# Ordering VectorE's weight work behind the gate chain and the residual additions at the out-projection openings of two FFNs, and reordering products of each first chunk

## The chip, the cores and the metric

One NeuronCore of a Trainium2 chip runs the whole kernel. The metric is the device time of one execution in microseconds (us). A separate execution was recorded by the hardware profiler; all rows of the profile come from it, and its times are counted from the first instruction. The engines are TensorE (PE, with its weight loads PEld), VectorE (DVE), ScalarE (ACT), GpSimd (POOL) and SyncE (SP), which issues most loads.

## The reference

The reference is one step of a two-layer streaming encoder over 512 prompt frames and 8 x 16 sample frames, 640 columns in all. Layer 0 is a Conformer convolution module, layer 1 attends to a shared K/V, and each is followed by a SwiGLU FFN. Everything is float32. Only the FFN matters here, with 1024 features and a hidden width of 2816:

```
def swiglu_ffn(h, g, w_in, w_out):
    a, b = jnp.split(rms_norm(h, g) @ w_in, 2, axis=-1)
    return h + (jax.nn.silu(a) * b) @ w_out
```

It is computed twice, once after each layer.

## The kernel before, in words

Features lie on the 128 partitions, frames along the rows. TensorE takes each float32 operand as two parts, `hi` (rounded to float32r) and `lo` (the rest), and a product of two is three matmuls: hi times hi, lo times hi, hi times lo (`product`, L436 to L445, matmul at L443). So every tile of weights must first be "cut": ScalarE writes hi (L375), VectorE subtracts to get lo (L376, `put`, L374). The gated values go through the same `put`; by their tiles the rows are told apart: `whi`, `wlo`, `shi`, `slo` are weights, `hid` gated values and `XH`, `XL` the FFN's input.

Most of each FFN multiplies 2 x 2 blocks with seven products instead of eight, named X11, X21, XT1, XT2, XT3, XT4 and X22. `w_seven` (L414) fetches one set of weights for that. SP loads four blocks into `raw` (two buffers); GpSimd loads one block into `s1` and adds another to it by DMA (L421, L422; two buffers too). Then VectorE makes sums in place, L426 (a21 = a11 + a21), L427 (a11 = s1 + a11) and L429 (a12 = a12 + a11), and each of the seven results is cut into a slot. There are 11 slots, used in turn.

Both FFNs (`ffn`, L337) go through 18 of the 22 tiles of hidden rows in three chunks. A chunk first has calls of `seven` (L528): six, but three in the first chunk, where three calls of another kind (`std`) stand ahead. A call makes a = W_a x and b = W_b x for one tile of hidden rows: 12 matmuls for each of the seven products. Products X11, XT2, XT3 and XT4 of a call add up in one accumulator, and ScalarE copies it out in between (`keep`, L455, after X11, XT2 and XT3). X21 is added to the first copy (`plus`, L460). Silu follows (L464), and the gate (`sink`, L502) multiplies (L480, L483), forms the sums that the second matrix needs (L483, L514, L522) and puts them into `hid`. The last two products of a call, XT4 and X22 (`after`, L546), are held over into the next call, or into the out-projection.

Then `out_chunk` (L559) multiplies the gated values of this chunk by its part of w_out, in four weight sets u = 0 to 3, again with seven products each, 9 matmuls in a product (three tiles of hidden rows, three matmuls each). Each finished accumulator is added to or subtracted from the residual `h` by VectorE (L584). The order on TensorE is written out by hand:

```
QORD = """50' a0 a1 10' 50" 10" 20 60' 30' 51' 60" 30" 51" 70 11 21 40 61 31 52 71 12 22 41 62 32 53 72
          13 23 42 63 33"""
```

The first digit is the product (5 XT1, 1 X11, 2 X21, 6 XT2, 3 X22, 7 XT3, 4 XT4), the second is u. One quote mark is the first six matmuls of the nine, two are the last three, which need the newest tile of hidden rows. `a0` and `a1` are the held-over XT4 and X22 of the last call (12 matmuls each); the last gated values come only from them. Products 7 and 4 of u = 3 (73, 43) are left for the first call of the next chunk. I call the stretch from 50' to about 70 the opening. Weights for u are fetched when QORD first names that u.

What is not written out by hand is ordered by a planner at compile time. It lists each engine's instructions by priority and by a model of when they are ready; `high_priority` raises a block. `tc.issue_after(i)` (in a helper, `behind`, L140) adds an edge: those instructions of the block that run on the same engine as `i` are listed after it. It is an order within one engine and adds no semaphore wait by itself. At run time each engine follows its list.

Of the kernel before, what the change touches and what calls it, by code (L numbers as in the profile page):

```python
# [60 lines left out]
X11, X21, XT2, XT1, XT3, XT4, X22 = range(7)  # L61
# [24 lines left out]
def tile_trunk(ctx, tc, xT, vecs, hist, w_pw1, w_pw2, w_in0, w_out0, w_os0, w_in1, w_out1, w_os1,  # L86
               w_kq, w_v, w_o, rel, kc, vc, y_out, convp_out, convs_out, k_out, v_out):
    nc = tc.nc
# [15 lines left out]
    def nm(s):  # L104
        uid[0] += 1
        return f"{s}_{uid[0]}"

    def mmt(n=512):
        return mm.tile([P, n], F32, tag="mm", name=nm("mm"))
# [29 lines left out]
    @contextmanager  # L139
    def behind(*ins):  # L140
        with ExitStack() as st:
            for i in ins:
                st.enter_context(tc.issue_after(i))
            yield
# [192 lines left out]
    def ffn(l, w_in, w_out, w_os, tail, hf, lead=(), b0=None, last_sum=()):  # L337
# [19 lines left out]
        lead, put_end = list(lead), [None, None]  # L357

        def ties():
            return lead.pop(0) if lead else ()  # L360
# [5 lines left out]
        sub, add, mult = ALU.subtract, ALU.add, ALU.mult  # L366
# [7 lines left out]
        def put(hi, lo, src):  # L374
            put_end[1] = nc.scalar.activation(out=hi, in_=src, func=AF.Copy).ins  # L375
            put_end[0] = nc.vector.tensor_tensor(out=lo, in0=src, in1=hi.bitcast(F32), op=sub).ins  # L376

        def cut(w, o, src):
            c = slice(o, o + src.shape[-1])
            put(w[0][:, c], w[1][:, c], src)  # L380

        def wraw():
            return wp.tile([P, 2048], F32, tag="raw", name=nm("raw"))
# [9 lines left out]
        def slot():  # L393
            turn[0] += 1
            hi, lo, o = slots[(turn[0] - 1) % len(slots)]
            return (hi, lo), o
# [14 lines left out]
                            cut(*ws[j // 512], raw[:, j:j + n])  # L411
            return ws[1], ws[0], ws[2], ws[3]

        def w_seven(src, out=False, first=(), rest=()):  # L414
            n = src.shape[-1] // 4
            raw, ws = wraw(), {}
            s1 = wx.tile([P, 512], F32, tag="s1", name=nm("s1"))[:, :n]
            nc.sync.dma_start(raw[:, :4 * n], src)
            a12, a11, a21, a22 = (raw[:, n * i:n * i + n] for i in range(4))
            with tc.high_priority(offset=HP), behind(*ties()):  # L420
                nc.gpsimd.dma_start(s1, src[:, 2 * n:3 * n])  # L421
                nc.gpsimd.dma_start(s1, src[:, 3 * n:4 * n], accum_op=add)  # L422
                for x in ((XT1, X11, X21, XT2, X22, XT3, XT4) if out else
                          (X11, X21, XT2, XT1, XT3, XT4, X22)):
                    if x == XT2:
                        nc.vector.tensor_tensor(out=a21, in0=a11, in1=a21, op=add)  # L426
                        nc.vector.tensor_tensor(out=a11, in0=s1, in1=a11, op=add)  # L427
                    elif x == X22:
                        nc.vector.tensor_tensor(out=a12, in0=a12, in1=a11, op=add)  # L429
                    ws[x] = slot()  # L430
                    with behind(*(first if x == XT1 else rest)):
                        cut(*ws[x], {XT1: s1, X11: a11, X21: a12, XT2: a11, X22: a12, XT3: a21,
                                     XT4: a22}[x])
            return ws

        def product(pt, w, xs, first, ks=None):  # L436
            (hi, lo), o0 = w
            n = len(xs)
            for k in ks or range(n):
                xh, xl = xs[k]  # L440
                c = slice(o0 + k * P, o0 + k * P + P)
                for i, (wt, v) in enumerate(((hi[:, c], xh), (lo[:, c], xh), (hi[:, c], xl))):
                    last = nc.tensor.matmul(pt, wt, v, start=(first and k == i == 0),  # L443
                                            stop=(k == n - 1 and i == 2), skip_group_check=True)
            return last  # L445

        def xproduct(pt, w, x, first):
            return product(pt, w, [(XH[x][:, k, :], XL[x][:, k, :]) for k in range(4)], first)

        keeps = []  # L450

        def keep(tag, pt):
            t = tp.tile([P, NH], F32, tag=tag, name=nm(tag))
            with tc.high_priority(offset=HP):
                keeps.append(nc.scalar.activation(out=t, in_=pt, func=AF.Copy).ins)  # L455
            return t

        def plus(t, pt):
            with tc.high_priority(offset=HP):
                nc.vector.tensor_tensor(out=t, in0=pt, in1=t, op=add)  # L460

        def silu(t, src):
            with tc.high_priority(offset=HP):
                nc.scalar.activation(out=t, in_=src, func=AF.Silu)  # L464
# [27 lines left out]
        def combined(HH, HL, kp, second, held, neg, early=None):  # L492
# [32 lines left out]
                        own(XT4, b21)  # L525
            return sink

        def seven(src, sink, before):  # L528
            ws = w_seven(src)
            pa, pb = mmt()[:, :NH], mmt()[:, :NH]  # L530
            xproduct(pa, ws[X11], X11, True)
            t1 = keep("t1", pa)
            before(0)
            xproduct(pb, ws[X21], X21, True)
            plus(t1, pb)
            silu(t1, t1)
            before(1)
            xproduct(pa, ws[XT2], XT2, False)
            t2 = keep("t2", pa)
            pe = mmt()[:, :NH]  # L540
            xproduct(pe, ws[XT1], XT1, True)
            xproduct(pa, ws[XT3], XT3, False)
            t3 = keep("t3", pa)
            plus(t3, pe)

            def after(i):  # L546
                if i == 0:
                    last = xproduct(pa, ws[XT4], XT4, False)
                    sink(0, t1, pa)
                else:  # L550
                    last = xproduct(pe, ws[X22], X22, False)
                    plus(t2, pe)
                    silu(t2, t2)
                    sink(1, t2, t3)
                return last

            return after

        def out_chunk(c, HH, HL, after):  # L559
            ws, pts = {}, {}  # L560
            prod = {5: ("e", XT1, True, 1, 1), 1: ("a", X11, True, 0, 0),
                    2: ("b", X21, True, 0, 0), 6: ("a", XT2, False, 1, 0),
                    3: ("e", X22, False, 1, 0), 7: ("a", XT3, False, 1, 1),
                    4: ("a", XT4, False, 0, 1)}

            def go(i, u, part):
                if u not in ws:
                    o = (4 * c + u) * 12 * P
                    ws[u] = w_seven(w_os[:, o:o + 12 * P], True,
                                    (keeps[2:3], keeps[-2:-1])[u] if c == 0 and u < 2 else (),  # L570
                                    keeps[-1:] if (c, u) == (0, 1) else ())
                b, x, first, half, row = prod[i]
                if first and part != '"':
                    pts[b, u] = mmt()[:, :NH]
                pt = pts[b, u]
                with tc.issue_after(last[0]) if last else nullcontext():
                    ins = product(pt, ws[u][x], list(zip(HH[x], HL[x])), first,
                                  {"": None, "'": (0, 1), '"': (2,)}[part])
                last[:] = [ins.ins]
                if part == "'":  # L580
                    return
                hv = h[:, 2 * u + row, half * NH:half * NH + NH]
                with tc.high_priority(offset=HP):
                    nc.vector.tensor_tensor(out=hv, in0=hv, in1=pt, op=sub if row else add)  # L584

            last = []
            for t in QORD.split():
                if t[0] == "a":
                    with tc.issue_after(last[0]):
                        last[:] = [after(int(t[1])).ins]  # L590
                else:
                    go(int(t[0]), int(t[1]), t[2:])
            return lambda i: go((7, 4)[i], 3, "")

        def stats(half):
            bc, _ = rstd_bc([h[:, k, half * NH:half * NH + NH] for k in range(KT)], NH, SQ, 6, None,
# [76 lines left out]
        for c in range(NCH):  # L673
            for jj in range(NSTD if c == 0 else 0, CW):
                if jj % 2 == 0:
                    held = [None] * 3
                if jj == NSTD and c == 0:
                    held = helds[1]
                after = seven(w_in[CW * c + jj], combined(HH, HL, jj // 2, jj % 2, held, True),
                              after)  # L680
            after = out_chunk(c, HH, HL, after)
            HH, HL = {}, {}
# [888 lines left out]
    for p in range(NP):  # L1571
# [8 lines left out]
        for op in BO[p].split():  # L1580
# [11 lines left out]
            i = int(op[1]) if len(op) > 1 else None  # L1592
            with pe(), tc.high_priority(offset=HP):
                if op[0] == "A":
# [4 lines left out]
                    pt = {hh: sp.tile([P, 1280], F32, tag="PT", name=nm("PT")) for hh in range(2)}  # L1599
# [22 lines left out]
    with tc.high_priority(offset=HP):  # L1622
        sqs = xp.tile([P, KT, 384], F32, tag="xl1", name=nm("sqs")).rearrange("p a n -> p (a n)")
        acc, r = sqs[:, KT * NH:(KT + 1) * NH], sqs[:, (KT + 1) * NH:(KT + 1) * NH + 8]
        for k in range(KT):
            sq = square(h[:, k, 0:NH], NH, "a", sqs[:, k * NH:(k + 1) * NH])
            if k:
                sq_end = nc.vector.tensor_tensor(out=acc, in0=acc if k > 1 else sqs[:, 0:NH],
                                                 in1=sq, op=ALU.add).ins
# [100 lines left out]
    last = [next(products) for _ in range(KT)][-1:]  # L1730
# [116 lines left out]
```

## Time and profile before

| what | value |
|---|---|
| time, median of 3 runs | 1443.44 us (1442.41 to 1444.12) |
| the profiled execution | 1440.09 us, span of its instructions 1438.3 us |
| TensorE busy | 1417.7 us (99% of the span), 11076 matmuls |
| VectorE busy | 1116.5 us (78%), 2490 instructions |
| ScalarE busy | 749.4 us (52%) |
| granted TensorE clock | 0.999 of full speed |

The first FFN runs from about 240 to 650 us of the span, the second from about 1000 to 1415. In a profile row the first number is the start, the second the duration, then engine, line, operation, output and inputs; in square brackets stands the time that the engine sat idle before it, and what ended that. In the list of waits a row gives who waited for whom, the total in us, how often, and the longest. Matmuls are pipelined: one of 128 x 320 is recorded as 0.31 us long though the next starts half as long after it.

### The profile page before, as it was taken

The page shows a single profiled execution, that of the slowest core. Times are in us where ns is not written, and L with a number is a line of the kernel's source. Part 1 is how long each engine was busy: PE and PEld are TensorE (multiplying, and loading weights), DVE is VectorE, ACT ScalarE, POOL GpSimd, SP SyncE. Part 2 cuts the span into 40 slices and gives each one's busy share as a digit, 9 for nine tenths or more (in the row PEclk, how much of TensorE's full clock was granted, in tenths as well). Part 3 has the DMA queues.
Part 4 walks back from the last instruction along what each step waited for, and adds up shares of the span by engine and source line. Part 5 has one row for each costly group of instructions (what it writes and reads, how often), then busy time and mean ns, then how long its engine had stood idle before and what let it go on. Part 6 is the DMA issues. An engine that isn't in the chain of part 4 may idle for free. (4 is left out here: it accounts for less than half of the span.)

```text
span 1438.3 us, 28229 instructions
## 1 busy us (share of the span) xinstructions
PE 1417.7 (99%) x11076; PEld 1363.5 (95%) x11076; DVE 1116.5 (78%) x2490; ACT 749.4 (52%) x1633; POOL 278.8 (19%) x335
## 2 busy tenths in 40 slices
PE   9999999999999999999999999999999999999998
PEld 9998799999999999999998998988999999999998
DVE  6799767988888889766666757667899788888855
ACT  5666554554554554545654544544564564554443
POOL 5699120011111111013111111110011111111101
PEclk9999999999999999999999999999999999999999
DMA  7267434055444445424455555561044534544512
GB/s 247 97 171 183 123 87 148 9 142 150 135 101 127 132 116 138 128 89 173 164 184 201 188 182 173 182 214 61 30 107 137 153 109 119 135 117 127 144 59 74
DMA packets 66933, 192.58 MB, mean 134 GB/s; under 512 B 12144, under 2 KB 30320, under 8 KB 58480
## 3 DMA queue, kind: packets, MB, share of 16 engines
q1 hardware_dynamic: 52432, 160.58, 34.4%
q0 software_dynamic: 13504, 29.37, 10.3%
q8 instruction: 87, 1.43, 0.4%
q10 hardware_dynamic: 864, 0.83, 0.2%
q14 instruction: 46, 0.38, 0.1%
HBM read 179.14 MB, written 11.61 MB: 133 GB/s over the span
## 5 line engine op out<-in xcount | busy, mean ns | idle before, releaser
L443 PE MATMUL mm<-XH,whi 128*128 128x320 f32 x896 | 275.6, 310 | 2.6 <-ACT t L455 2.6
L443 PE MATMUL mm<-XH,wlo 128*128 128x320 f32 x896 | 276.3, 309 | 0.0
L443 PE MATMUL mm<-XL,whi 128*128 128x320 f32 x896 | 274.7, 309 | 0.0
L375 ACT ACTIVATE whi<-raw 128x512 fp32r<-128x512 f32 (+2 forms) x280 | 169.0, 614 | 139.7 <-PE mm L443 113.3
L376 DVE TENSOR_TENSOR wlo<-raw,whi 128x512 fp32r<-128x512 f32 (+2 forms) x280 | 184.2, 666 | 21.2 <-ACT whi L375 20.2
L443 PE MATMUL mm<-hid,whi 128*128 128x320 f32 x732 | 171.9, 310 | 3.4 <-DVE hid L376 2.7
L443 PEld LDWEIGHTS mm<-XH,whi 128*128 128x128 f32 x896 | 167.8, 188 | 4.2 <-ACT t L455 4.2
L443 PEld LDWEIGHTS mm<-XH,wlo 128*128 128x128 f32 x896 | 168.2, 188 | 0.0
L443 PEld LDWEIGHTS mm<-XL,whi 128*128 128x128 f32 x896 | 167.8, 188 | 0.0
L443 PEld LDWEIGHTS mm<-hid,whi 128*128 128x128 f32 x732 | 124.8, 188 | 6.0 <-DVE hid L376 3.7
L202 PE MATMUL mm<-xh,whi 128*128 128x320 f32 (+2 forms) x416 | 128.8, 312 | 0.8 <-DVE h L706 0.4
L203 PE MATMUL mm<-xh,wlo 128*128 128x320 f32 (+2 forms) x416 | 128.0, 309 | 0.0
L204 PE MATMUL mm<-xl,whi 128*128 128x320 f32 (+2 forms) x416 | 125.6, 310 | 0.4 <-DVE xl L192 0.4
L443 PE MATMUL mm<-hid,wlo 128*128 128x320 f32 x366 | 113.0, 309 | 0.0
L443 PE MATMUL mm<-XH,shi 128*128 128x320 f32 x344 | 105.9, 309 | 0.7 <-DVE h L1560 0.7
L443 PE MATMUL mm<-XH,slo 128*128 128x320 f32 x344 | 106.0, 308 | 0.0
L443 PE MATMUL mm<-XL,shi 128*128 128x320 f32 x344 | 105.5, 308 | 0.0
L421 POOL DMA_DIRECT2D s<-in_w_in x38 | 22.0, 579 | 374.3 <-DVE wlo L376 149.7
L852 POOL TENSOR_TENSOR ca<-ca,cvt 128x512 f32<-128x512 f32 x60 | 89.7, 1494 | 17.0 <-ACT cvt L849 10.8
L375 ACT ACTIVATE shi<-raw 128x512 fp32r<-128x512 f32 (+1 forms) x114 | 66.4, 588 | 43.9 <-PE mm L443 39.0
L455 ACT ACTIVATE t<-mm 128x320 f32<-128x320 f32 x114 | 49.6, 435 | 67.3 <-PE mm L443 66.6
L584 DVE TENSOR_TENSOR h<-h,mm 128x320 f32<-128x320 f32 x168 | 79.6, 479 | 4.9 <-PE mm L443 4.7
(337 smaller groups left out, 3683.4 us busy)
## 6 DMA issues: line engine op xcount, KB each, us to landing
raw<-in_w_in SPq DMA_DIRECT2D x38, 1024.0 KB
s<-in_w_in POOLq DMA_DIRECT2D x76, 256.0 KB, 4.0
raw<-in_w_os SPq DMA_DIRECT2D x24, 768.0 KB
cache<-in_ck SPq DMA_DIRECT2D x32, 512.0 KB
cache<-in_cv SPq DMA_DIRECT2D x32, 512.0 KB
raw<-in_w_pw SPq DMA_DIRECT2D x11, 1024.0 KB
s<-in_w_os POOLq DMA_DIRECT2D x48, 192.0 KB, 3.6
raw<-in_w_kq SPq DMA_DIRECT2D x8, 1024.0 KB
```

Source lines behind the costliest of these rows:

```text
L202: nc.tensor.matmul(ps, wh, xh, start=(first and i == 0), stop=False)
L203: nc.tensor.matmul(ps, wl, xh, start=False, stop=False)
L204: end = nc.tensor.matmul(ps, wh, xl, start=False, stop=(stop and i == last))
L375: put_end[1] = nc.scalar.activation(out=hi, in_=src, func=AF.Copy).ins
L376: put_end[0] = nc.vector.tensor_tensor(out=lo, in0=src, in1=hi.bitcast(F32), op=sub).ins
L421: nc.gpsimd.dma_start(s1, src[:, 2 * n:3 * n])
L443: last = nc.tensor.matmul(pt, wt, v, start=(first and k == i == 0), stop=(k == n - 1 and i == 2), skip_group_check=True)
L455: keeps.append(nc.scalar.activation(out=t, in_=pt, func=AF.Copy).ins)
L584: nc.vector.tensor_tensor(out=hv, in0=hv, in1=pt, op=sub if row else add)
L852: nc.gpsimd.tensor_tensor(out=acc, in0=acc, in1=pr, op=ALU.add)
```

## The change

Nothing is added to or taken from the computation; no instruction, load or buffer differs in number or size. Edges are added:

- In `w_seven`, the sums (L426, L427, L429) now stand inside the `behind` block of the cut that follows them, and there is a new edge, `late`, for every result that isn't named in `soon`. Since `late` names VectorE instructions, it binds the sums and the lo subtractions, not ScalarE's hi.
- In `out_chunk`, `late` is: nothing for u = 0; for u = 1 the last `put` of the gate chain that follows a1, with XT1, X11 and X21 free (`soon`); for u = 2 the residual addition of product 70; for u = 3 that of product 22.
- The first call of `seven` after a chunk has its XT2, XT3, XT4 and X22 work behind the addition of product 33, the second behind that of product 43; X11, X21 and XT1 are free.
- On TensorE, in the first chunk, XT1 of the second call is listed behind XT2 of the first, and XT1 of the third call behind its own XT2. In every chunk the first product of the out-projection (50') is listed behind XT3 of the last call.

```
@@ -411,7 +411,7 @@
                             cut(*ws[j // 512], raw[:, j:j + n])
             return ws[1], ws[0], ws[2], ws[3]
 
-        def w_seven(src, out=False, first=(), rest=()):
+        def w_seven(src, out=False, first=(), rest=(), late=(), soon=()):
             n = src.shape[-1] // 4
             raw, ws = wraw(), {}
             s1 = wx.tile([P, 512], F32, tag="s1", name=nm("s1"))[:, :n]
@@ -422,15 +422,16 @@
                 nc.gpsimd.dma_start(s1, src[:, 3 * n:4 * n], accum_op=add)
                 for x in ((XT1, X11, X21, XT2, X22, XT3, XT4) if out else
                           (X11, X21, XT2, XT1, XT3, XT4, X22)):
-                    if x == XT2:
-                        nc.vector.tensor_tensor(out=a21, in0=a11, in1=a21, op=add)
-                        nc.vector.tensor_tensor(out=a11, in0=s1, in1=a11, op=add)
-                    elif x == X22:
-                        nc.vector.tensor_tensor(out=a12, in0=a12, in1=a11, op=add)
                     ws[x] = slot()
-                    with behind(*(first if x == XT1 else rest)):
-                        cut(*ws[x], {XT1: s1, X11: a11, X21: a12, XT2: a11, X22: a12, XT3: a21,
-                                     XT4: a22}[x])
+                    with behind(*(() if x in soon else late),
+                                *(first if x == XT1 else rest)):
+                        if x == XT2:
+                            nc.vector.tensor_tensor(out=a21, in0=a11, in1=a21, op=add)
+                            nc.vector.tensor_tensor(out=a11, in0=s1, in1=a11, op=add)
+                        elif x == X22:
+                            nc.vector.tensor_tensor(out=a12, in0=a12, in1=a11, op=add)
+                        cut(*ws[x], {XT1: s1, X11: a11, X21: a12, XT2: a11, X22: a12,
+                                     XT3: a21, XT4: a22}[x])
             return ws
 
         def product(pt, w, xs, first, ks=None):
@@ -525,8 +526,15 @@
                         own(XT4, b21)
             return sink
 
+        xt2_end, xt3_end, chunk_add = [], [None], []
+
+        def tie(own):
+            xt2_end.append(own)
+            return {2: xt2_end[:1], 3: xt2_end[2:]}.get(len(xt2_end), ())
+
         def seven(src, sink, before):
-            ws = w_seven(src)
+            ws = w_seven(src, late=chunk_add[:1], soon=(X11, X21, XT1))
+            chunk_add[:1] = ()
             pa, pb = mmt()[:, :NH], mmt()[:, :NH]
             xproduct(pa, ws[X11], X11, True)
             t1 = keep("t1", pa)
@@ -535,11 +543,12 @@
             plus(t1, pb)
             silu(t1, t1)
             before(1)
-            xproduct(pa, ws[XT2], XT2, False)
+            own = xproduct(pa, ws[XT2], XT2, False).ins
             t2 = keep("t2", pa)
             pe = mmt()[:, :NH]
-            xproduct(pe, ws[XT1], XT1, True)
-            xproduct(pa, ws[XT3], XT3, False)
+            with behind(*tie(own)):
+                xproduct(pe, ws[XT1], XT1, True)
+            xt3_end[0] = xproduct(pa, ws[XT3], XT3, False).ins
             t3 = keep("t3", pa)
             plus(t3, pe)
 
@@ -557,7 +566,7 @@
             return after
 
         def out_chunk(c, HH, HL, after):
-            ws, pts = {}, {}
+            ws, pts, hadd, hid_end = {}, {}, {}, []
             prod = {5: ("e", XT1, True, 1, 1), 1: ("a", X11, True, 0, 0),
                     2: ("b", X21, True, 0, 0), 6: ("a", XT2, False, 1, 0),
                     3: ("e", X22, False, 1, 0), 7: ("a", XT3, False, 1, 1),
@@ -568,7 +577,9 @@
                     o = (4 * c + u) * 12 * P
                     ws[u] = w_seven(w_os[:, o:o + 12 * P], True,
                                     (keeps[2:3], keeps[-2:-1])[u] if c == 0 and u < 2 else (),
-                                    keeps[-1:] if (c, u) == (0, 1) else ())
+                                    keeps[-1:] if (c, u) == (0, 1) else (),
+                                    ((), hid_end, hadd.get((7, 0)), hadd.get((2, 2)))[u],
+                                    (XT1, X11, X21)[:3 * (u == 1)])
                 b, x, first, half, row = prod[i]
                 if first and part != '"':
                     pts[b, u] = mmt()[:, :NH]
@@ -581,16 +592,25 @@
                     return
                 hv = h[:, 2 * u + row, half * NH:half * NH + NH]
                 with tc.high_priority(offset=HP):
-                    nc.vector.tensor_tensor(out=hv, in0=hv, in1=pt, op=sub if row else add)
-
-            last = []
+                    hadd[i, u] = [nc.vector.tensor_tensor(out=hv, in0=hv, in1=pt,
+                                                          op=sub if row else add).ins]
+
+            last = [xt3_end[0]]
             for t in QORD.split():
                 if t[0] == "a":
                     with tc.issue_after(last[0]):
                         last[:] = [after(int(t[1])).ins]
+                    hid_end[:] = put_end[:1]
                 else:
                     go(int(t[0]), int(t[1]), t[2:])
-            return lambda i: go((7, 4)[i], 3, "")
+            chunk_add[:] = hadd[3, 3]
+
+            def rest(i):
+                go((7, 4)[i], 3, "")
+                if i:
+                    chunk_add[:] = hadd[4, 3]
+
+            return rest
 
         def stats(half):
             bc, _ = rstd_bc([h[:, k, half * NH:half * NH + NH] for k in range(KT)], NH, SQ, 6, None,
```

## Prediction

> **What bounds the kernel.** I read the page first, then the list of who TensorE waited for, then the timelines of TensorE and VectorE around those waits.
>
> ```profile
> span 1438.3 us, 28229 instructions
> ...
> PE 1417.7 (99%) x11076; PEld 1363.5 (95%) x11076; DVE 1116.5 (78%) x2490; ACT 749.4 (52%) x1633; POOL 278.8 (19%) x335
> ...
> L455 ACT ACTIVATE t<-mm 128x320 f32<-128x320 f32 x114 | 49.6, 435 | 67.3 <-PE mm L443 66.6
> ...
> s<-in_w_os POOLq DMA_DIRECT2D x48, 192.0 KB, 3.6
> ```
>
> TensorE is busy 99% of the span, and the change neither adds nor removes a matmul. So it can only win what TensorE loses between matmuls, and it loses if it makes new gaps. TensorE's waits by releaser, whole run:
>
> ```profile
> PE mm L443 <- DVE hid L376: 3.7, 6, 1.0
> PE mm L443 <- ACT t L455: 2.6, 6, 0.5
> ...
> PE mm L443 <- DVE h L584: 0.9, 2, 0.7
> ...
> PE mm L443 <- ACT hid L375: 0.3, 1, 0.3
> ```
>
> The columns are total us, times, longest. All fifteen lie in the two FFN stages. Two of the six on L455 (0.3 and 0.2 us, the list asked for in the windows 625 to 635 and 1390 to 1400) stand in the closing products, which the change doesn't touch:
>
> ```profile
> PE mm L443 <- ACT t L455: 0.3, 1, 0.3
> PE mm L443 <- ACT t L455: 0.2, 1, 0.2
> ```
>
> That leaves 2.1 us in four waits on L455, two in the first chunk of each FFN, and 3.7 + 0.9 + 0.3 = 4.9 us in nine waits at the six out-projection openings. The change reorders work around exactly these thirteen, 7.0 us by this list.
>
> The list shows too little, however. TensorE's rows around one wait of each kind (the first and the last of the four on L455 among them):
>
> ```profile
> 294.40 0.41 PE L443 MATMUL mm<-XH,whi 128*128 128x320 f32 x1 [0.53 <-ACT t L455]
> ...
> 1058.75 0.31 PE L443 MATMUL mm<-XL,shi 128*128 128x320 f32 x1
> 1059.58 0.42 PE L443 MATMUL mm<-XH,whi 128*128 128x320 f32 x1 [0.53 <-ACT t L455]
> 1059.84 0.32 PE L443 MATMUL mm<-XH,wlo 128*128 128x320 f32 x1
> 1059.99 0.31 PE L443 MATMUL mm<-XL,whi 128*128 128x320 f32 x1
> ...
> 1079.05 0.31 PE L443 MATMUL mm<-hid,whi 128*128 128x320 f32 x1
> ...
> 1079.93 0.31 PE L443 MATMUL mm<-XH,whi 128*128 128x320 f32 x1
> ...
> 1082.38 0.42 PE L443 MATMUL mm<-XH,whi 128*128 128x320 f32 x1 [0.53 <-ACT t L455]
> ...
> 1204.71 0.31 PE L443 MATMUL mm<-hid,wlo 128*128 128x320 f32 x1
> 1205.60 0.56 PE L443 MATMUL mm<-hid,whi 128*128 128x320 f32 x2 [0.58 <-DVE hid L376]
> 1206.00 0.30 PE L443 MATMUL mm<-hid,wlo 128*128 128x320 f32 x1
> ```
>
> Undisturbed, the six matmuls of 50' from 1079.05 to 1079.93 take 0.88 us: a pace of 0.147 us. From 1058.75 to 1059.99 there are three steps and 1.24 us, 0.80 more than 3 x 0.147; the list counts 0.53 of it. From 1204.71 to 1206.00 three steps (the row x2 is two matmuls) take 1.29 us, 0.85 too much; the list counts 0.58. So each wait costs 0.27 us beyond its entry. [...]
>
> **The products of the first chunk.** ScalarE copies an accumulator out (L455) before the next product adds to it. From the last matmul of one product to the first of the next this takes 1059.58 - 1058.75 = 0.83 us, 0.68 more than the pace, unless other products stand between. The change puts XT1 of the second call behind XT2 of the first, and XT1 of the third behind its own XT2. Each is 12 matmuls, 1.76 us, between an XT2 and the XT3 that waits for the copy. The other wait, at 1082.38, comes since 50' (six matmuls, from 1079.05) stands ahead of the XT3 at 1079.93, which leaves XT3 and XT4 side by side; 50' now comes behind XT3 and covers the 0.68 us with 0.88, a margin of 0.2 us. No work is added. What ran behind the XT1 that is moved comes up by 1.76 us, and the rows of the first call's XT2 must be ready that much earlier. I take them to be, as VectorE waits there for ScalarE and not the reverse:
>
> ```profile
> 1060.08 0.69 DVE L376 TENSOR_TENSOR slo<-raw,shi 128x512 fp32r<-128x512 f32 x1 [2.17 <-ACT shi L375]
> ```
>
> VectorE idles 2.17 us since the slot it is to fill is freed by that XT2, so an earlier XT2 also helps VectorE. Gain: 2.1 + 4 x 0.27 = 3.2 us; bounds 0 (a new gap opens elsewhere) and 3.2.
>
> **The openings.** I follow the worst one, second chunk of the first FFN. a1 has ended when 10' begins at 432.98. TensorE from there with its two waits, then VectorE (shortened), then ScalarE's silu:
>
> ```profile
> 432.98 0.32 PE L443 MATMUL mm<-hid,whi 128*128 128x320 f32 x1
> ...
> 436.91 0.41 PE L443 MATMUL mm<-hid,whi 128*128 128x320 f32 x1 [0.69 <-DVE h L584]
> ...
> 441.13 0.56 PE L443 MATMUL mm<-hid,whi 128*128 128x320 f32 x2 [1.03 <-DVE hid L376]
> ```
> ```profile
> 433.77 0.56 DVE L426 TENSOR_TENSOR raw<-raw 128x384 f32<-128x384 f32 x1 [1.40 <-DMA raw<-in_w_os]
> 434.24 0.55 DVE L429 TENSOR_TENSOR raw<-raw 128x384 f32<-128x384 f32 x1
> ...
> 435.11 0.48 DVE L460 TENSOR_TENSOR t<-mm,t 128x320 f32<-128x320 f32 x1
> 435.51 0.55 DVE L376 TENSOR_TENSOR slo<-raw,shi 128x384 fp32r<-128x384 f32 x1
> 435.98 0.88 DVE L584 TENSOR_TENSOR h<-h,mm 128x320 f32<-128x320 f32 x2
> 436.78 0.48 DVE L483 SCALAR_TENSOR_TENSOR B<-t,t 128x320 f32<-128x320 f32 x1
> 437.18 1.02 DVE L376 TENSOR_TENSOR wlo<-raw,whi 128x384 fp32r<-128x384 f32 x2
> ...
> 439.72 0.55 DVE L376 TENSOR_TENSOR wlo<-raw,whi 128x384 fp32r<-128x384 f32 x1
> ...
> 440.60 1.28 DVE L376 TENSOR_TENSOR hid<-B,hid 128x320 fp32r<-128x320 f32 x3
> ```
> ```profile
> 435.63 0.47 ACT L464 ACTIVATE t<-t 128x320 f32<-128x320 f32 x1 [2.31 <-DVE t L460]
> ```
>
> The gate chain needs only t (L460), ScalarE's silu, gate (L483), subtraction (L483), cast and hid (L376). Yet VectorE first waits 1.40 us for a load, for rows that no product needs for 15 us, then does six operations on rows of u=1 and u=2 ahead of the hids at 440.60 (L426, L429, slo and three wlo), 0.47 us apart. All are what the change ties behind the end of the chain (u=1) or behind the addition of 70 (u=2). Without them the chain runs so. Of the 0.83 us above, 0.15 is pace and 0.44 the copy, so handing over both ways takes 0.25; t can thus start at 433.2 instead of 435.11, the silu (0.47) ends at 434.2; both h additions and the gate by 435.8; then subtraction, the next B, an h addition, hid of X22, subtraction and hid of XT2 in steps of 0.4 us (435.11 to 435.51), done by 438.3. The product that waits, 60", would reach its third matmul 41 steps after a1, at 432.98 + 41 x 0.147 = 439.0. Slack 0.7 us, and the h addition that 60' needs comes by 435.4, its turn at 436.1. Both waits go. The other five openings share 4.9 - 1.7 = 3.2 us by the list, a smaller hold-up of the same kind, so I take the whole term: 4.9 + 9 x 0.27 = 7.3 us; bounds 0 and that.
>
> What is pushed back: u=1's seven operations, 7 x 0.47 = 3.3 us behind the chain, so done about 10 us after a1; the first user, 61, comes 84 steps or 12.4 us after a1, and needs only the third of them. u=2's wait for the addition of 70 (57 steps, 8.4 us, plus about 0.7); 52 comes at 102 steps, 15.0 us. u=3's wait for 22 (138 steps, 20.4 + 0.7 = 21.1 us); 53 comes at 165 steps, 24.3 us: the thinnest cover, 3.2 us for one 0.55 us subtraction. The next chunk's XT2 comes 42 steps, 6.2 us, behind 33; its two additions, cast and subtraction take 4 x 0.6 = 2.4 us. Loads move too: SP's next raw load waits for u=1's last cut and GpSimd's pair for s1 waits for L427, so both start up to 10 us after a1; u=3 uses them from 24.3 us on, against 2 x 3.6 us to landing for the pair. I cost all this at nothing; without that cover each late row would cost its own 0.5 us in each chunk. A small gain lies here as well, not in the sum: the next chunk's L426, waiting for its load, held up two additions and TensorE:
>
> ```profile
> 1219.92 0.69 DVE L426 TENSOR_TENSOR raw<-raw 128x512 f32<-128x512 f32 x1 [1.08 <-DMA raw<-in_w_in]
> ```
> ```profile
> 1221.28 0.73 PE L443 MATMUL mm<-hid,whi 128*128 128x320 f32 x2
> 1221.85 0.31 PE L443 MATMUL mm<-hid,wlo 128*128 128x320 f32 x1
> ```
>
> Two steps take 0.57 instead of 0.295, 0.28 lost; at most six times, 1.7 us.
>
> **Sum.** 3.2 + 7.3 = 10.5 us. The profiled execution took 1440.09 us (span 1438.3 and 1.8 around it), 3.35 below the median of 1443.44. It would take 1429.6, and the median 1432.9.
>
> **Rivals.** *The chain is latency.* It goes to and fro between ScalarE and VectorE; if that set the openings, only the products' 3.2 us would come: 1440.2. Against it stands that six operations and a 1.40 us wait lie inside. 0.10.
>
> *Half an opening.* The order on VectorE comes from a planner. If it sets u=0's rows or u=1's first three (untied) into the chain, or the 0.2 and 0.7 us margins fail, about half of 7.3 stays: 1436.5. 0.15.
>
> *Late rows, slower.* VectorE can't work ahead any more: it idles until 22's and 33's additions and must then do ten operations for u=3, the h additions and the next chunk's rows at once.
>
> ```profile
> 1120.00:1195.00 75.00, 75.00 (x513) 75.00 (x512) 61.02 (x117) 42.11 (x88) 9.98 (x14) 1.00 0.47 123
> 1195.00:1240.00 45.00, 44.38 (x300) 43.70 (x299) 38.97 (x84) 19.91 (x39) 4.83 (x7) 1.00 0.50 143
> ```
>
> (Columns: stretch, its us, then busy us of TensorE, weight loads, VectorE.) In the chunk from 1195 to 1240 VectorE has 45 - 38.97 = 6.0 us to spare, in the 75 us before it 14.0. If the ties make it idle over 6.0 us in a chunk, TensorE pays; from 10.5 / 6 = 1.75 us beyond that in each of six chunks the change loses. With u=3's first product 2.5 us late each time (five operations in front of its row) it is 15 - 10.5 = 4.5 us slower: 1447.9. By this the first product to wait is 53. Against it: the slack of 3.2 us there, and that VectorE is rid of its waits of 1.40 and 2.17 us. 0.08. [...]
>
> *It changes nothing.* Each tie only orders an engine's own list; if the planner's list had that order, nothing moves: 1443.4. The rows above speak against it. 0.07.
>
> **Numbers.** Forecast 0.60, half 0.15, latency 0.10, slower 0.08, nothing 0.07. About 0.2%, 2.9 us, can be told from no change. Faster: 0.60 + 0.15 + 0.07 of the latency case, which lies on that edge: 0.82; same 0.03 + 0.07 = 0.10; slower 0.08. The forecast's own range is 1430.3 (with the 1.7 us, and 0.9 for the spread of the runs) to 1435; the range reaches to the latency case, 1440.3.
>
> **What would show it.** Right: the list of TensorE's waits keeps only the two closing L455 entries; the rows around the first chunk's XT3 show no 0.53; in an opening L460 starts 0.25 us after a1 with no raw, slo or wlo of u=1's last four before the third hid. Wrong: waits on wlo, slo or h at 53, at XT2 of a chunk's first call, or VectorE idle before L584 with TensorE waiting behind it.

## The result, and the profile after

The changed kernel takes 1431.97 us (median of 5 runs, 1430.44 to 1434.54) against 1443.44 us before (5 runs, 1441.49 to 1444.12): a ratio of 0.9928, 95% interval 0.9917 to 0.9938. That is 11.5 us less; a second set of runs (below) gave 10.4 us. The forecast was 1432.9 us. The profiled execution took 1433.02 us. Three executions that ran slower as a whole, two of the kernel before (1538 and 2322 us) and the profiled one of the experiment with u = 1 and u = 2 (2813 us), are left out of all medians and of the loss defined below.

The page of the changed kernel, span and busy times (lines after the gate now have other numbers: the matmul is L444, `keep` L456, `plus` L461, silu L465, the gate L484, the addition to `h` L595, the sums of weights L429, L430 and L432):

```profile
span 1431.2 us, 28185 instructions
...
PE 1416.2 (99%) x11076; PEld 1364.0 (95%) x11076; DVE 1113.0 (78%) x2490; ACT 744.1 (52%) x1633; POOL 277.8 (19%) x335
```

The same matmuls, the same work on VectorE, and 7.1 us less span. The list of TensorE's waits (who waited for whom, total us, times, longest), only the rows of the FFN products (one more, 0.7 us on an addition at the start of the second FFN, stands in both kernels and lies outside the change):

```profile
PE mm L444 <- ACT t L456: 0.7, 3, 0.3
...
PE mm L444 <- ACT whi L375: 0.6, 1, 0.6
...
PE mm L444 <- DVE h L595: 0.4, 2, 0.2
```

No wait on `hid` is left. To compare kernels I use one more number, the *loss*: over the two FFNs from their first matmul up to their closing products (the first 2616 matmuls of `product` in each), every step from one matmul's start to the next that is more than 0.03 us over the pace of 0.147 us, the excess added up. Before it was 7.3 + 7.3 = 14.6 us, after 2.7 + 4.6 = 7.3 us. Of these, 1.5 and 1.8 us lie at the start of the FFNs, where nothing was changed.

VectorE in the opening that the prediction followed (second chunk of the first FFN; a1 ends when 10' begins on TensorE, at 431.71):

```profile
431.91 0.49 DVE L461 TENSOR_TENSOR t<-mm,t 128x320 f32<-128x320 f32 x1 [0.24 <-PE mm L444]
432.94 0.49 DVE L484 SCALAR_TENSOR_TENSOR B<-t,t 128x320 f32<-128x320 f32 x1 [0.54 <-ACT t L465]
433.35 0.88 DVE L595 TENSOR_TENSOR h<-h,mm 128x320 f32<-128x320 f32 x2
...
436.15 1.29 DVE L376 TENSOR_TENSOR hid<-B,hid 128x320 fp32r<-128x320 f32 x3
437.36 0.55 DVE L429 TENSOR_TENSOR raw<-raw 128x384 f32<-128x384 f32 x1
```

`plus` starts 0.20 us after a1, and nothing on weights stands between it and the three hids; the first sum of u = 1 follows at 437.36. The hids are done 437.44 - 431.71 = 5.7 us after a1, 41 matmuls or 6.0 us after a1 they are needed.

Three small losses are new. First, in each opening, 70 waits for the addition of 60": two operations on rows of u = 1, which may run as soon as the chain has ended, stand in front of it. VectorE and TensorE in the first opening of the second FFN:

```profile
1085.97 0.55 DVE L429 TENSOR_TENSOR raw<-raw 128x384 f32<-128x384 f32 x1
1086.44 0.55 DVE L376 TENSOR_TENSOR slo<-raw,shi 128x384 fp32r<-128x384 f32 x1
1086.90 0.48 DVE L595 TENSOR_TENSOR h<-h,mm 128x320 f32<-128x320 f32 x1
```
```profile
1086.92 0.31 PE L444 MATMUL mm<-hid,whi 128*128 128x320 f32 x1
1087.44 0.41 PE L444 MATMUL mm<-hid,whi 128*128 128x320 f32 x1 [0.20 <-DVE h L595]
```

The step of 0.52 us is 0.37 too long, with 0.11 in the next. This happens in the two first-chunk openings; in the other four it is 0.18. Second, 0.24 us in the first call after each chunk, six times: its XT2 and XT3 have only four matmuls between them. Third, once, a load for the third call of the second chunk of the second FFN landed late. VectorE, then TensorE:

```profile
1130.23 0.69 DVE L429 TENSOR_TENSOR raw<-raw 128x512 f32<-128x512 f32 x1 [0.92 <-DMA raw<-in_w_in]
```
```profile
1131.01 0.38 PE L444 MATMUL mm<-XH,whi 128*128 128x320 f32 x1
1132.01 0.42 PE L444 MATMUL mm<-XH,whi 128*128 128x320 f32 x1 [0.62 <-ACT whi L375]
1132.69 0.41 PE L444 MATMUL mm<-XH,whi 128*128 128x320 f32 x1 [0.26 <-ACT t L456]
```

Two steps take 1.68 us, 1.4 too long.

### The profile page after: what moved, and what is told of

Read it like the earlier page. It is cut to its first block, busy times and chain, and to the rows that moved or that the text cites. A ratio compares the mean times of both kernels' runs of the same rounds, so it can differ in the third digit from the quotient of the medians.

```text
span 1431.2 us, 28185 instructions
## 1 busy us (share of the span) xinstructions
PE 1416.2 (99%) x11076; PEld 1364.0 (95%) x11076; DVE 1113.0 (78%) x2490; ACT 744.1 (52%) x1633; POOL 277.8 (19%) x335
## 3 DMA queue, kind: packets, MB, share of 16 engines
q0 software_dynamic: 13504, 29.37, 10.5%
## 5 line engine op out<-in xcount | busy, mean ns | idle before, releaser
L444 PE MATMUL mm<-XH,wlo 128*128 128x320 f32 x896 | 276.3, 309 | 0.0
L444 PE MATMUL mm<-XH,whi 128*128 128x320 f32 x896 | 274.7, 310 | 1.4 <-ACT t L456 0.7
L444 PE MATMUL mm<-XL,whi 128*128 128x320 f32 x896 | 275.0, 309 | 0.0
L444 PE MATMUL mm<-hid,whi 128*128 128x320 f32 x732 | 170.7, 310 | 0.4 <-DVE h L595 0.4
L444 PEld LDWEIGHTS mm<-XH,whi 128*128 128x128 f32 x896 | 167.5, 188 | 3.4 <-ACT t L456 2.4
L444 PEld LDWEIGHTS mm<-XH,wlo 128*128 128x128 f32 x896 | 168.2, 188 | 0.0
L444 PEld LDWEIGHTS mm<-XL,whi 128*128 128x128 f32 x896 | 167.8, 188 | 0.0
L444 PEld LDWEIGHTS mm<-hid,whi 128*128 128x128 f32 x732 | 124.7, 188 | 1.8 <-DVE h L595 1.3
L595 DVE TENSOR_TENSOR h<-h,mm 128x320 f32<-128x320 f32 x168 | 79.2, 481 | 46.1 <-PE mm L444 46.0
L444 PE MATMUL mm<-hid,wlo 128*128 128x320 f32 x366 | 113.0, 309 | 0.0
L444 PE MATMUL mm<-XH,shi 128*128 128x320 f32 x344 | 106.1, 310 | 0.7 <-DVE h L1580 0.7
L444 PE MATMUL mm<-XH,slo 128*128 128x320 f32 x344 | 106.0, 308 | 0.0
L444 PE MATMUL mm<-XL,shi 128*128 128x320 f32 x344 | 105.5, 308 | 0.0
L202 PEld LDWEIGHTS mm<-xh,whi 128*128 128x128 f32 x416 | 78.0, 188 | 3.3 <-ACT xh L190 1.5
```

What stands on the lines that cost most here:

```text
L202: nc.tensor.matmul(ps, wh, xh, start=(first and i == 0), stop=False)
L595: hadd[i, u] = [nc.vector.tensor_tensor(out=hv, in0=hv, in1=pt, op=sub if row else add).ins]
```

## The experiments

All but the first are variants of the changed kernel. The kernel before ran beside each set: 1442.13 us (first four rows), 1442.85 us (next four) and 1442.01 us (last four). The loss is from one profiled execution of each.

| kernel | median, us | ratio to before, interval | loss, us |
|---|---|---|---|
| before, again | 1442.39 | 1.0002, 0.9993 to 1.0010 | 14.8 |
| TensorE's ties alone | 1439.98 | 0.9987, 0.9979 to 0.9996 | 14.0 |
| VectorE's ties alone | 1435.47 | 0.9953, 0.9941 to 0.9965 | 10.6 |
| all but the next chunk's ties | 1433.38 | 0.9943, 0.9931 to 0.9955 | 7.7 |
| the change, again | 1432.43 | 0.9929, 0.9917 to 0.9941 | 6.5 |
| tie of u = 1 alone | 1442.20 | 0.9998, 0.9990 to 1.0007 | 15.8 |
| tie of u = 2 alone | 1439.91 | 0.9981, 0.9972 to 0.9990 | 14.0 |
| change with three mends | 1441.28 | 0.9993, 0.9983 to 1.0003 | 14.3 |
| u = 1 and u = 2 | 1438.34 | 0.9970, 0.9958 to 0.9982 | - |
| u = 1 and u = 3 | 1443.95 | 1.0014, 1.0004 to 1.0025 | 18.1 |
| change, chunk behind 23 | 1431.90 | 0.9932, 0.9920 to 0.9945 | 5.2 |
| the same, XT1 later | 1430.25 | 0.9919, 0.9906 to 0.9933 | 4.5 |

Against the kernel before in its own set, every variant gains 0.4 to 2.4 us more by its median than by its loss (14.8 in the repeat of before). The loss shows which waits came and went in one execution; what a variant is worth is read from the medians.

### How steady the kernel before is

No edit.

> The kernel before, unchanged, for a second profile of it. The change gained 11.5 us by medians but 7.1 by the two profiled spans, as the profiled execution of before (1440.09) lay 3.35 us under its median. Theory (a load that lands late stops VectorE's list inside the openings, by a different amount in each execution): times again spread over 1441 to 1444, and a profiled execution near 1443 shows 2 to 4 us more of waits at the openings than the 4.9 us of the first profile, behind longer waits of VectorE's L426 on raw. Rival (a profiled execution of this program is simply about 3 us short): profile again near 1440, medians near 1443.4, the same 4.9 us of waits.

Its profiled execution took 1441.41 us, 1.0 below its median, where the first lay 3.35 below. Waits move between openings (the worst gap was now 1.18 us in the third opening of the first FFN), while their sum stays: 3.9 us on hid against 3.7, and the loss 14.8 us against 14.6. So the distance of a profiled execution from the median is scatter and not the constant that the rival assumed. But the theory isn't borne out either: this execution's span is 1.3 us longer with hardly longer waits at the openings, and 1.0 us of that lies between the two FFNs.

### The two halves of the change

TensorE's ties alone (no `late`):

```
-                    with behind(*(() if x in soon else late),
-                                *(first if x == XT1 else rest)):
+                    with behind(*(first if x == XT1 else rest)):
```

> Only TensorE's ties: XT1 of the first chunk's second and third calls, and 50' behind XT3; no tie on VectorE's weight work. Theory: the four waits of 0.53 us on L455 in the two first chunks go, the waits at the openings stay: 3.2 us faster than before, 1440.2. Rival (the products moved only uncover other gaps): 1443.4. Rival (half of the gain of the whole change is the products): 1437.5.

VectorE's ties alone:

```
-            return {2: xt2_end[:1], 3: xt2_end[2:]}.get(len(xt2_end), ())
+            return ()
...
-            last = [xt3_end[0]]
+            last = []
```

> Only VectorE's ties (u = 1, 2, 3 and the two calls after a chunk); TensorE's ties left out. Theory: the waits at the openings go and the four of 0.53 us on L455 in the first chunks stay, or return in part: 3.2 us slower than the whole change, 1435.2. Rival (the chain is latency): 1440 or more, waits on hid left.

The waits of the first, then of the second:

```profile
PE mm L443 <- DVE hid L376: 4.6, 6, 1.4
...
PE mm L443 <- DVE h L594: 2.2, 5, 1.1
...
PE mm L443 <- ACT t L455: 0.5, 2, 0.3
```
```profile
PE mm L444 <- ACT t L456: 3.2, 9, 0.5
...
PE mm L444 <- DVE h L595: 0.2, 1, 0.2
```

Both times come out as forecast, 1439.98 for 1440.2 us and 1435.47 for 1435.2. Each half removes its own kind. With TensorE's ties only the two closing waits on the copy are left, but the openings wait 6.8 us (4.6 + 2.2) instead of 5.0 in the repeat of before: part of what the products gain is given back there, 2.2 us net instead of 3.2. By starts the openings lose 12.3 us instead of 9.9. With VectorE's ties no wait on hid is left, 6.7 us, while the copies still wait; by starts the openings lose 2.1 us. The halves add up to 8.8 us, the whole gives 10.4; the intervals are too wide to call the rest a joint gain.

### The next chunk's ties

The first two calls after a chunk untied:

```
-            ws = w_seven(src, late=chunk_add[:1], soon=(X11, X21, XT1))
+            ws = w_seven(src, late=(), soon=(X11, X21, XT1))
```

> The whole change without the ties of the first two calls behind the additions of products 33 and 43 (u = 1, 2, 3 and TensorE's ties stay). The profile after shows a new wait of about 1.5 us in the second FFN's second chunk, with a raw load that landed late after the buffer was freed late, and VectorE idle for 2.7 and 2.6 us before it. Theory (that wait is the price of these ties): it goes, while next-chunk sums again wait for their load inside the chunk's last products, about 0.3 us in each: 1431.0 to 1432.5, within 1 us of the whole change. Rival (these ties carry part of the gain): 1434 or more.

At 1433.38 us the run misses the theory's range by 0.9 us and lies short of the rival's 1434. The late load is gone from this profile, but the copy of an accumulator makes TensorE wait in seven places, two of them in the closing products:

```profile
PE mm L444 <- ACT t L456: 2.1, 7, 0.4
```

The two kernels' intervals overlap (0.9931 to 0.9955 and 0.9917 to 0.9938), so with the rest of the change in place these ties are worth some 2 us by the medians (8.8 us gained without them, 10.4 and 11.5 with them), not clear of the noise. Nor do the next chunk's sums wait as the theory had it: in 33 us around and behind each of the six openings, VectorE waits for a load once, 0.24 us, and TensorE loses 0.1 us at most behind it.

### The change once more

> The whole change again, to stand on the same chip and in the same rounds as the kernels beside it. If the gain of the parts adds up (products 2.2 us and VectorE's ties 6.7 us as measured one by one), it is 8.9 us faster than before, 1433.2; by the first comparison it was 11.5 us. A profile with the wait of 1.5 us behind a late raw load in the second FFN's second chunk again means that it is part of the order; without it, that it is a matter of one execution.

1432.43 us, 10.4 less than before. The profiled execution took 1432.43 us too, and its late load cost 0.6 us, at another place (371.51 us) than the first; it held up ScalarE by 1.95 us, and with it a copy. So a late load turned up in both executions of the change, at different places.

### Which of VectorE's ties does it

The chain is held up by rows of u = 1 and u = 2, as the prediction says. I took u = 1's tie for the larger part. In all of these, TensorE's ties and those of the next chunk are off, as above; then, for u = 1 alone:

```
-                                    ((), hid_end, hadd.get((7, 0)), hadd.get((2, 2)))[u],
+                                    ((), hid_end, (), ())[u],
```

> Only the tie of u = 1 behind the gate chain; u = 2, u = 3, the calls after a chunk and TensorE are left as before. Theory (the chain is held up by weight operations that stand inside it, most of them of u = 1): the waits on hid go except where u = 2's first sum waits for its load; about 5 of VectorE's 6.7 us: 1437. Rival (the waiting load is what matters): 1440 or more, waits on hid hardly smaller.

For u = 2 alone the line reads `((), (), hadd.get((7, 0)), ())[u]`.

> Only the tie of u = 2 behind the addition of product 70. One sum of 0.47 us and its load wait leave each opening, the operations of u = 1 stay. Theory: each opening shortens by 0.47 us and the worst by its load wait too, 2 to 3.5 us in all: 1439.4. Rival (the waiting load is what matters): 1437 or less.

My theory falls: u = 1 alone gains nothing. Its list of waits shows why that isn't the same as doing nothing:

```profile
PE mm L444 <- DVE h L595: 4.9, 11, 0.9
PE mm L444 <- ACT t L456: 2.6, 6, 0.5
```

The waits on hid went, and eleven waits on additions came. Its VectorE in the first opening, and TensorE beside it:

```profile
339.46 0.88 DVE L595 TENSOR_TENSOR h<-h,mm 128x320 f32<-128x320 f32 x2
342.14 0.56 DVE L429 TENSOR_TENSOR raw<-raw 128x384 f32<-128x384 f32 x1 [1.80 <-DMA raw<-in_w_os]
342.78 0.56 DVE L376 TENSOR_TENSOR wlo<-raw,whi 128x384 fp32r<-128x384 f32 x1
343.25 0.48 DVE L595 TENSOR_TENSOR h<-h,mm 128x320 f32<-128x320 f32 x1
```
```profile
343.06 0.31 PE L444 MATMUL mm<-hid,whi 128*128 128x320 f32 x1
343.79 0.42 PE L444 MATMUL mm<-hid,shi 128*128 128x320 f32 x1 [0.42 <-DVE h L595]
```

VectorE waits 1.80 us for the load of u = 3, with an addition behind it in its list, and TensorE loses 0.58 us on that addition. The load is late since it goes into the buffer that u = 1 gives back. SP's issue of it, in the kernel before and in this one:

```profile
325.62 0.33 SPq L418 DMA_DIRECT2D raw<-in_w_os  x1
```
```profile
336.03 0.33 SPq L418 DMA_DIRECT2D raw<-in_w_os  x1
```

It starts 10.4 us later, 0.9 of them because this execution reaches the FFN later. The same pair (a VectorE wait on u = 3's load, then a loss on TensorE within 1.2 us) stands in all six openings of this run. So u = 1's tie moves the trouble from the chain to the first row behind it that isn't tied. The tie of u = 2 holds back no load that early (the first row on u = 3's load starts within 1.1 us of its time before in all six openings, in the first at 331.58 us for 331.55), and gains 2.9 us by itself, as forecast.

Which partner does u = 1 need? With u = 2:

> Only the ties of u=1 (behind a1's last cut) and of u=2 (behind the addition of 70); u=3, the next chunk's calls and TensorE's order as before. Theory: the tie of u=1 alone gained nothing because u=1's buffer comes free later, so the load of u=3 lands later (342.14 us in that run's first opening) while u=3's sum, which isn't tied, stands ahead of an addition. The tie of u=2 doesn't mend that. The six waits on hid left with u=2 alone (about 0.9 us each with what follows them, 5.4 us) go, and six waits on an addition behind the load of u=3, about 0.8 us each (5.0 us in the run of u=1 alone), come: about 1439.5 us, within 1.5 us of u=2 alone. Rival: u=1's late rows only changed places with u=2's, so both together are the gain: 1435.5 us, all that VectorE's ties gave together, and no VectorE wait on the load of u=3 ahead of an addition that TensorE waits for.

With u = 3, `((), hid_end, (), hadd.get((2, 2)))[u]`:

> Only the ties of u=1 (behind a1's last cut) and of u=3 (behind the addition of 22); u=2, the next chunk's calls and TensorE's order as before. Theory (u=3 must stand behind its additions once u=1 is tied): the waits on hid stay away and so do the six additions behind the load of u=3, 5.0 us less than u=1 alone: 1437.2 us, range 1435.5 to 1438.5. Rival (u=1 changed places with u=2): the tie of u=3 frees nothing by itself, 1442.2 us as with u=1 alone, with waits on h of 4 us or more in the list of waits.

With u = 2 the ratio is 0.9970, a gain of 3.7 us. The rival's 1435.5 us lies outside its interval and the theory's 1439.5 at its upper edge; which waits are left in it is not shown. With u = 3 the forecast fails: the run is 1.9 us slower than before, not 5 us faster. Its profile:

```profile
345.31 0.69 DVE L429 TENSOR_TENSOR raw<-raw 128x512 f32<-128x512 f32 x1 [0.98 <-DMA raw<-in_w_in]
345.92 0.55 DVE L376 TENSOR_TENSOR wlo<-raw,whi 128x384 fp32r<-128x384 f32 x1
346.39 0.48 DVE L595 TENSOR_TENSOR h<-h,mm 128x320 f32<-128x320 f32 x1
```
```profile
346.90 0.31 PE L444 MATMUL mm<-hid,whi 128*128 128x320 f32 x1
347.80 0.42 PE L444 MATMUL mm<-hid,whi 128*128 128x320 f32 x1 [0.59 <-DVE h L595]
```

u = 3's sum waits for no load there any more, but now the next chunk's first load (`in_w_in`) is waited for ahead of an addition, and TensorE loses 0.75 us. Five of the six openings have this pair. SP issues that load hardly later than before (337.82 us against 337.47), but only 3.2 us behind the load of u = 3, where 11.9 us lay between them before, and the first operation on it starts 7.5 us after its issue instead of 5.3. In the five openings the figures are 3.2 to 3.3 and 7.3 to 7.5 us, in the six of before 9.5 to 11.9 and 5.3 to 5.6. What makes that stretch longer no run shows. So the lateness has gone on by one more row, to the one that is still untied. That was in my theory's reach, and I left it out of the number. Much of the 18.1 us of loss is in waits on copies, 6.1 us in this run's list against 2.6 with u = 1 alone: the planner's order of the products came out less favourable too, which I haven't taken apart.

In 33 us around and behind each of the six openings of the kernel before, VectorE waits for a load of `raw` 14 times, 11.2 us together; with u = 1 alone 11 times, 13.9 us; with u = 2 alone 12 times, 14.0 us; with u = 1 and u = 3 11 times, 11.8 us. With the whole change it doesn't once. The ties of u = 2 and u = 3 without that of u = 1 were not run, so that u = 1's is needed rests on the waits on `hid` that u = 2 alone leaves (3.0 us in its list).

### Mending the new losses

Three mends at once: u = 1's last four results deferred behind the addition of 60" (traced after it), the chunk's first call behind 23 instead of 33, and that call's XT1 behind its own XT2.

```
-                                    ((), hid_end, hadd.get((7, 0)), hadd.get((2, 2)))[u],
+                                    ((), None, hadd.get((7, 0)), hadd.get((2, 2)))[u],
...
+                if (i, u) == (6, 0):
+                    more[0](hadd[6, 0])
...
-            chunk_add[:] = hadd[3, 3]
+            chunk_call[0] = 0
+            chunk_add[:] = hadd[2, 3]
```

> The whole change, and three mends of what its profile shows: u = 1's late rows are bound behind the addition of 60 at the end instead of the chain's end, so that 70 does not wait for that addition (0.47 us in each first chunk, about 0.2 in the others); XT1 of the first call after a chunk is listed behind its own XT2 (0.24 us, six times); that call's late rows are bound behind the addition of 23 instead of 33, so that the raw buffer is free four products sooner (1.5 us once). Theory: 2.5 to 4 us faster than the whole change. Rival (VectorE then idles elsewhere and the waits only move): the same within 1 us.

It is 9 us slower than the change, which neither the theory nor the rival had. Waits, then VectorE and TensorE in the first opening:

```profile
PE mm L458 <- DVE wlo L376: 6.5, 6, 1.1
```
```profile
331.75 0.55 DVE L436 TENSOR_TENSOR raw<-raw 128x384 f32<-128x384 f32 x1
332.22 0.48 DVE L613 TENSOR_TENSOR h<-h,mm 128x320 f32<-128x320 f32 x1
...
334.50 0.87 DVE L613 TENSOR_TENSOR h<-h,mm 128x320 f32<-128x320 f32 x2
335.29 0.55 DVE L376 TENSOR_TENSOR wlo<-raw,whi 128x384 fp32r<-128x384 f32 x1
```
```profile
334.35 0.45 PE L458 MATMUL mm<-hid,whi 128*128 128x320 f32 x2
335.89 0.41 PE L458 MATMUL mm<-hid,wlo 128*128 128x320 f32 x1 [1.09 <-DVE wlo L376]
```

u = 1's last sum (here L436) now runs at 331.75 us instead of 329.40 in the repeat of the change, and its rows come after products 61 and 31 want them: 2.2 us lost in each opening, 13.0 us in all, to save 1.7. A row that is pushed too far back costs more than the addition in front of which it stood.

The mends of the chunk without the deferral: first only the addition,

```
-            chunk_add[:] = hadd[3, 3]
+            chunk_add[:] = hadd[2, 3]
```

> The whole change, with the late rows of the first call after a chunk tied behind the addition of 23 instead of 33, which comes earlier. Theory: the load of the third call after a chunk, which cost 1.5 us in the profile of the change and 0.6 us in its second profile, waits for the buffer that these rows hold, so it starts earlier and that wait goes: 0.6 to 1.5 us less than the change, 1430.9 to 1431.8 us. Rival: the landing scatters by itself, and the time stays that of the change, 1432.4 us, with such a wait left in the profile.

then with XT1 of that call behind its XT2 as well (`behind(*tie(own), *([own] if lone else []))`, `lone` true in a chunk's first call):

> The run before (23 instead of 33) and, in the first call after a chunk, XT1's product behind XT2's own, so that the copy of t2 is covered by XT1's products and not by the 4 small ones alone. Theory: the six losses of 0.24 us at these calls go as well, 1.4 us: 1429.5 to 1430.4 us. Rival: XT1's product, now later, makes its own copy late, and a wait on the addition to t3 (L461) or on the silu behind it takes their place: 1431 us or more.

SP's issue of the third call's load in the second FFN, in the changed kernel and with 23:

```profile
1125.13 0.33 SPq L418 DMA_DIRECT2D raw<-in_w_in  x1
```
```profile
1116.14 0.33 SPq L418 DMA_DIRECT2D raw<-in_w_in  x1
```

The load starts 9.0 us earlier, and TensorE doesn't wait for it. The six losses of 0.24 us are gone too, already here and not only with XT1 tied: with 23 the planner by itself lists some thirty matmuls of other products between XT2 and XT3. So the second mend has nothing left to mend, and its time lies in the range forecast for another reason; the two FFNs take 790.0 and 790.1 us from their first to their last matmul of `product`. The medians, 1431.90 (0.1 us above the range forecast) and 1430.25 us, differ by about what the runs scatter. Both are at or a little below the change, and the last is the fastest kernel tried, 11.8 us less than before; that it beats the change isn't settled (0.9906 to 0.9933 against 0.9917 to 0.9938).

## Why the prediction was right

*The time and the sum.* Forecast 10.5 us, measured 11.5 and 10.4. All thirteen waits are gone, and counting by starts was right: the products lost 3.2 us, where the list has 2.1. The sum was not complete, though. More went than it held: the openings of before lost 9.8 us by starts, additions held up behind the next chunk's load among them, against 7.3. And something came: 2.5 us in the openings (0.48 twice and 0.18 four times on the addition of 60", smaller ones behind), 1.4 us in the first calls, 0.6 to 1.5 us of late load. By the loss the net is 7.3 us, in the repeats 8.4 (14.8 - 6.5, rounded); the profiled executions differ by 7.1 and 9.0 us, so the loss accounts for them. The medians show 2 to 4 us more, and no trace shows where: the two profiled executions of before lay 3.4 and 1.0 us below their medians. That the forecast meets the medians to 1 us is therefore in part luck: in the traces 13.0 us went and some 5 came, where the sum had 10.5 and 0.

*Products, 3.2 us.* The four waits are gone, and the 0.2 us of margin for 50' held. Alone the step gives 2.2 us, and the openings lose more.

*Openings, 7.3 us.* VectorE's ties alone give 6.7 us. The timing of the chain was close: hids 5.7 us after a1 where 5.3 was worked out, and 6.0 needed, so the slack was 0.3 us and not 0.7. What failed is a part of the working: "I cost all this at nothing", of the rows pushed back, is right only of the set. The tie of u = 1 by itself costs as much as it gains, through the buffer that it holds. u = 1 and u = 2 together reach 3.7 of the 6.7 us; with u = 3 as well, and TensorE's ties, it is 8.8 us without the next chunk's ties. So the tie of u = 3, to which the sum gave no gain, is worth about 3 us beside the other two (estimated from 8.8 - 2.2 - 3.7), while the next chunk's ties add some 2 us, not clear of the noise.

*The rivals.* The chain isn't latency: it was left as it is, and with VectorE's ties alone the openings lose 2.1 us instead of 9.9. No half of an opening stayed either, as no wait on `hid` is left. Of the late rows, nothing waits at 53, the place that this rival named, but they did appear once in each profile, with the load for the third call of a chunk: 0.6 to 1.5 us.

*The profile's offset.* The profiled execution was put 3.35 us below the median. The repeat was 1.0 below; after, the profiled execution was 1.0 above. The forecast used the offset on both sides, so it dropped out.

## What to carry to other kernels

A tie that pushes an engine's work back also pushes back the buffer that it frees and the load that goes there (with the tie of u = 1 alone, 10.4 us later, 0.9 of them since the FFN is reached later): follow that load to the first operation that waits for it, and see what is queued behind. Here work on loaded rows belonged behind the short operations for which TensorE, the bound engine, waits, and on each set in turn: a single tie handed the wait to the next one, and it ended once all of u = 1 to 3 were tied, with or without the next chunk's. And push no row further than its first user allows: to save 0.48 us twice and 0.18 four times cost 2.2 us six times.

## What the runs showed of the hardware

I had not expected that the wait on a load would be so costly at second hand. In the kernel before, each of these was 0.25 to 1.48 us on VectorE, and VectorE ran nothing else meanwhile. A later load didn't change the order on these engines: from 316 to 380 us 107 operations of VectorE stand in the same order in both profiled executions of the change, and from 340 to 380 us 34 of ScalarE, though one of these waited 0.91 us for its load in the first execution and 1.95 us in the second. In the run of u = 1 alone the addition of 343.25 stood behind the wait that ended at 342.14, and that addition is what TensorE lost time on. A load of u = 3's rows took 342.14 - 336.03 = 6.1 us from its issue to the first operation on it. Clock and pace didn't differ: 0.997 to 1.000 granted and 0.147 us from matmul to matmul in every profiled execution for which a loss is given.
